# Three heads' values, the chain outputs and the second norm's factors turned by VectorE and by transfers through DRAM

## The chip, the cores and the metric

The kernel runs on one core of one Trainium2 chip. The metric is the device time of one execution in microseconds, the median of several runs. Engines are named as in the profile: PE is TensorE's products, PEld its weight loads, DVE is VectorE, ACT is ScalarE, POOL is GpSimd, SP is SyncE, which issues the DMAs.

## The reference

One layer of a hybrid decoder over a sequence of 1024 tokens of width 1024, all in float32. An RMS norm and one input projection feed two mixers. Mixer A is a gated DeltaNet with four heads of 128; mixer B is an attention with eight heads of 64 over three dilated windows. Their outputs side by side go through one output projection and are added to the input. A second RMS norm follows, a gated MLP of width 2816 with a short causal convolution, and a last RMS norm. Cut to what the change touches:

```python
h = rmsnorm(x, norm1_w)
proj = h @ w_in
qkv_a = silu(causal_dwconv(qkv_a, conv_qkv_w))
qa, ka, va = l2norm(q) * 128 ** -0.5, l2norm(k), v
o_a = gated_delta_rule(qa, ka, va, g, beta)          # chunked, a state of 128 x 128 per head
o_a = rmsnorm(o_a, gdn_norm_w) * silu(z)
x = x + concatenate([o_a, o_b], -1) @ w_out
h = rmsnorm(x, norm2_w)
u = causal_dwconv(h @ w_up, ffn_conv_w)
x = x + (silu(gate) * up) @ w_down
return rmsnorm(x, final_norm_w)
```

## The kernel before

**Layout.** Activations lie transposed: 128 channels on the partitions, 1024 tokens along the free dimension. Products of full precision are made of three products of split operands (`mm3`: high times high, high times low, low times high). `half(h)` is a half of 512 tokens. The mixers' chains need some operands by token instead, so tiles of 128 x 128 are transposed by TensorE against an identity matrix (`tp`), which lands in a PSUM bank, and then copied to SBUF.

**What sets the order.** A planner (`Weave`) runs generators, called streams, each with a level; it keeps its own estimate of time for TensorE (`wv.pe`), for each engine and for each tile's readiness. An `Engine` object wraps an engine with a fixed price and a price per element, and for the queues with a time to land: `sy` is the SP queue at 0.05 us, 0.00142 us an element of a partition's row and 2.2 us to land. `wv.need(tile)` is the time until the planner expects the tile; `yield` with that lets other streams go first. The order of TensorE's instructions is fixed to the order in which the streams issue them. The orders of the other engines and of the queues are made by a scheduler with a simulation of its own, where `uv` and `ua` are VectorE and ScalarE with urgency. Every engine works its queue in order. Tiles of one tag share a ring of slots; `t2` is two deep.

**The stages.** `dense` takes the projection's columns in the order of `DENSE`: keys, attention values, then q and v of each head in turn, the attention's columns, and last the gate columns z. Each column is 48 products. Beside it, at more urgent levels, run `kprep`, `qprep` and `vprep` for each head. When the keys of all heads are done, `forward_sub` solves 32 x 32 triangles on VectorE, and `merges` joins them to 128 x 128 in the visits listed in `VISITS` (steps a, b, c, d for each head, with copies `w1` and `w2` in the ring `t2`); a visit waits for its operands and MSLACK more. `chain(h)` then steps through eight chunks of 128 tokens. The state recurrence makes it a sequence of short products and VectorE operations, and the four heads' chains are interleaved. A chain ends with a multiplication by GpSimd, then comes `finish`. `attention` starts when all four outputs are finished. The gate columns z fill TensorE's time beside the attention. `out_proj`, `mlp_up` (with a Strassen scheme of seven products P1 to P7 for each channel tile) and `mlp_down` follow.

**The three places of the change.**
- `vprep(h, vT)`: `tokens` transposes the eight pieces of a head's values and ScalarE scales each with the key norm on its way from PSUM to `vtok`, the tile that the chain reads, and later overwrites with its output.
- `finish(h, osb)`: eight transposes of the head's output, a copy by ScalarE with the norm weight (`gw2`), a store to `mixer[h]` in DRAM. At column z of the head it is read back into `og` and multiplied by the gate.
- `rms2_power` and `rms2_spread`: the sums of squares by token (a product with ones), GpSimd's power, then eight transposes of a factor column broadcast over 128 columns, and two copies to `rstdB`, which holds the factors on every partition. They are called in `up` for the first channel tile: `rms2_power` between P6 and P7, after the last quarter of P2, and `rms2_spread` after P7.

Of the kernel before, what the change touches and what calls it, by code (L numbers as in the profile page):

```python
# [10 lines left out]
OP = mybir.AluOpType  # L11
# [136 lines left out]
def hybrid_layer(tc, I, out):  # L148
# [6 lines left out]
    ua = Engine(wv, nc.scalar, "scalar", 0.12, 0.00085, first=tc.high_priority)  # L155
    po_ = Engine(wv, nc.gpsimd, "gpsimd", 0.15, 0.0021)
    sy = Engine(wv, nc.sync, "sync", 0.05, 0.00142, 2.2)
    sa = Engine(wv, nc.scalar, "actq", 0.05, 0.00142, 2.2)
    es = ExitStack()
    cp = es.enter_context(tc.tile_pool(name="cp", bufs=1))  # L160
# [6 lines left out]
    def tile_(pool, shape, dt, name, tag, bufs):  # L167
        return wv.slot(pool.tile(list(shape), dt, name=name, tag=tag, bufs=bufs), tag, bufs)
# [3 lines left out]
    def A(name, tag, dt=F32, shape=(P, 1024)):  # L172
        if tag in TURNS:
            i = turns[tag] = turns.get(tag, -1) + 1
            tag = TURNS[tag][i % len(TURNS[tag])]
        return tile_(lp, shape, dt, name, tag, SLOTS[tag])
# [19 lines left out]
    def tp(dst, src, idt=None, us=0.11):  # L196
        tc.stamp_issue_order_token(nc.tensor.transpose(dst, src, ident if idt is None else idt).ins, TOKEN)  # L197
        wv.product(us, dst, src)
# [61 lines left out]
    qpark = dp.tile([H, P, S], F32, name="qpark")  # L260
    atpark = dp.tile([H, P, S], F32, name="atpark")
    ddram = dp.tile([7, 8, P], F32, name="ddram")
    xpark = dp.tile([KT, P, S], F32, name="xpark")
    upark = dp.tile([FT, P, S], F32, name="upark")

# [3 lines left out]
    def next_bank(tag, *tiles, slack=0.0):  # L269

        while max(wv.need(*tiles), wv.slot_free(tag, 2)) + slack > 1e-3:
            yield max(wv.need(*tiles), wv.slot_free(tag, 2)) + slack
        return bank(tag)

    def half(i):
        return slice(i * 512, i * 512 + 512)
# [236 lines left out]
    def silu2(xr, name):  # L513
        y = A(name, "ev")
        ac.activation(y, xr, AF.Tanh, scale=0.5)
        ve.scalar_tensor_tensor(y, y, 1.0, xr, op0=OP.add, op1=OP.mult)
        return y
# [15 lines left out]
    def dense():  # L533

        yield from wv.until("first")
        yield from wv.until("norms")
        wv.add(2, first_keys())

        srcs, tiles = [], 0
        for col in DENSE:  # L540
            if col[0] == "V":
                srcs += [I["wv"][j] for j in range(4)]
            else:
                srcs.append(I["wi"][tiles])
                tiles += 1
        place = [0]
        raw = [raw_weight(srcs[0])]
        nxt = [weight(None, st=raw.pop())]
        raw.append(raw_weight(srcs[1]))

        def take():
            w = nxt.pop()
            i = place[0] = place[0] + 1
            if i < len(srcs):
                nxt.append(weight(None, st=raw.pop(), spare=i >= 17))
            if i + 1 < len(srcs):
                raw.append(raw_weight(srcs[i + 1]))
            return w

        def values_by_token(g):  # L560

            banks = [bank(t) for t in ("asc", "asc", "ch", "ch")]
            for j in range(4):
                w = [t.rearrange("p (k m) -> p k m", k=2) for t in take()]
                for kk in range(2):
                    k = 2 * j + kk
                    for i, pt in enumerate(banks):
                        c = 4 * g + i
                        yield wv.need(pt, *w)
                        mm3(pt, [t[:, c * P:(c + 1) * P] for t in xs[k]], [t[:, kk, :] for t in w], k == 0, k == KT - 1)  # L570
            for i in range(0, 4, 2):
                vx = A("vx", "ev", shape=(P, 2, 512))
                for e in range(2):
                    c = 4 * g + i + e
                    ac.activation(vx[:, e, :], banks[i + e], AF.Copy, scale=rst[:, c:c + 1])
                c = 4 * g + i
                sy.dma_start(vpark[c * P:(c + 2) * P].rearrange("(e p) d -> p e d", e=2), vx)
            wv.done.add(("V", g))

        for i, col in enumerate(DENSE):  # L580
            kind, h = col[:2]
            if kind == "V":
                yield from values_by_token(h)
                continue
            if kind == "z":
                yield from wv.until(("o", h))
            w = [t.rearrange("p (k m) -> p k m", k=KT) for t in take()]
            pair = []
            for hh in range(2):
                pt = bank("hf")  # L590
                yield wv.need(pt, *w)
                for k in range(KT):
                    mm3(pt, [t[:, k, :] for t in w], [t[:, half(hh)] for t in xs[k]], k == 0, k == KT - 1)
                    yield 0.0

                pair.append(pt)
                if hh == 0:
                    xr = A("aqkv" if kind == "a" else "xr", "go" if kind == "k" else "ev")
                scaled(pair, "xr", kind == "a", t=xr, hs=(hh,))
            if kind == "k":  # L600
                T["k", h] = conv_silu(xr, 4 + h, "kT", "kT*")
                wv.add(3, kprep(h))
            elif kind == "q":
                q = conv_silu(xr, h, "qT", "qa")
                wv.add(4, qprep(h, q))
            elif kind == "v":
                v = conv_silu(xr, 8 + h, "vT", "qa")
                wv.add(4, vprep(h, v))
            elif kind == "z":
                og = gated[h] = A("og", "kT*")  # L610
                sy.dma_start(og, mixer[h])
                ve.tensor_tensor(og, og, silu2(xr, "zz"), op=OP.mult)
            else:
                sy.dma_start(apark[h, col[2]], xr)
                wv.done.add(col)
        wv.done.add("dense")
# [83 lines left out]
    def qprep(h, qT):  # L700
# [22 lines left out]
        d.update(rq=rq, gq=gq)  # L723
        wv.done.add(("q", h))

    def vprep(h, vT):
        yield from wv.until(("q", h))
        yield wv.need(vT, slack=SLACK)
        G[h]["vtok"] = yield from tokens(vT, A("vtok", ("dv", "dw")[h % 2]), G[h]["nk"])
        wv.done.add(("v", h))  # L730

    def forward_sub():
# [179 lines left out]
        wv.add(1, finish(h, vtok))  # L912

    def finish(h, osb):
        for hh in range(2):
            pt = yield from next_bank("atr", osb)
            for c in range(4):
                i = 4 * hh + c
                tp(pt[:, c * P:(c + 1) * P], osb[:, i * P:(i + 1) * P])
            ot = tile_(sp, [P, 512], F32, "ot", "t2", 2)  # L920
            ac.activation(ot, pt, AF.Copy, scale=gw2)
            sy.dma_start(mixer[h][:, half(hh)], ot)
        wv.done.add(("o", h))


# [21 lines left out]
    def attention():  # L947
# [56 lines left out]
        def turn(pair):  # L1004
# [26 lines left out]
            if g["n"] < 7 and pair[1]["u"] == 3:  # L1031
                dt = tile_(sp, [P, 32], F32, "dt", "dt", 2)
                ve.transpose(dt, dns[g["n"] % 2])
                to = ddram[g["n"]]
                for b in range(4):
                    sy.dma_start(to[:, 32 * b:32 * b + 32], dt[32 * b:32 * b + 8, :])
                rT = g["rT"] = tile_(sp, [P, 512], F32, "rT", "t2", 2)
                for e, er in enumerate(HALVES):
                    src = to.rearrange("(u e) t -> e u t", e=2)[e]
                    sy.dma_start(rT[er].rearrange("p (u t) -> p u t", u=4),  # L1040
                                 bass.AP(tensor=src.tensor, offset=src.offset, ap=[[0, 64]] + list(src.ap)))

        def spread(pair):
# [216 lines left out]
    def rms2_power():  # L1260
        ps = bank("atr")
        for c in range(NCH):
            mm(ps[:, c:c + 1], rstdB[:, c * P:(c + 1) * P], ones[:, :1], 0.215)
        rs = sp.tile([P, NCH], F32, name="rs")
        uv.tensor_scalar(rs, ps[:, :NCH], 1.0 / 1024, EPS, op0=OP.mult, op1=OP.add)
        rsqrt(rs, rs, NCH)
        return rs

    def rms2_spread(rs):
        for h in range(2):  # L1270
            pb = bank("atr")
            for c in range(4):
                tp(pb[:, c * P:(c + 1) * P], rs[:, 4 * h + c:4 * h + c + 1].to_broadcast([P, P]))
            ve.tensor_copy(rstdB[:, half(h)], pb)

    W = {}
    raws = {}
# [62 lines left out]
    def up(n, before):  # L1340
# [15 lines left out]
        u2 = tile_(wp, [P, 512], F32, "u2", "wlo", 2)  # L1356
        last["u2"] = ac.activation(u2, pa, AF.Copy)
        if before is None:
            yield from up_product(n, "P2", pd, False, ks=(3,))
            rs = rms2_power()  # L1360
        else:
            yield from up_product(n, "P5", pc, True, False)
        yield from up_product(n, "P7", pa, False, False)
        if before is None:
            rms2_spread(rs)
        else:
            pd = yield from next_bank("hf")
            yield from up_product(n, "P2", pd)
# [346 lines left out]
```

## Time and profile before

| | us |
|---|---|
| median of 3 runs (1196.92 to 1198.09) | 1197.95 |
| the profiled execution's own time | 1197.51 |
| its span in the trace | 1195.7 |
| TensorE busy | 1183.8 |
| VectorE busy | 915.7 |
| ScalarE busy | 571.0 |
| GpSimd busy | 82.1 |
| granted TensorE clock, mean | 0.997 |

Busy times are sums over one profiled execution. The span runs from its first to its last instruction; the execution's own time is a little longer. A group's row gives line, engine, operation, written tile and read tiles with their shapes, the count, then busy time in us and mean duration in ns, then the idle time of the engine just before, with what ended it. A row of the timeline gives start, duration, engine, line and instruction. Most rows of VectorE and ScalarE have line 142 or 144, those of the wrapper, and TensorE's 193 (products) and 197 (transposes), so rows are found by tile names.

### The profile page before, as it was taken

The page shows a single profiled execution, that of the slowest core. Times are in us where ns is not written, and L with a number is a line of the kernel's source. Part 1 is how long each engine was busy: PE and PEld are TensorE (multiplying, and loading weights), DVE is VectorE, ACT ScalarE, POOL GpSimd, SP SyncE. Part 2 cuts the span into 40 slices and gives each one's busy share as a digit, 9 for nine tenths or more (in the row PEclk, how much of TensorE's full clock was granted, in tenths as well). Part 3 has the DMA queues.
Part 4 walks back from the last instruction along what each step waited for, and adds up shares of the span by engine and source line. Part 5 has one row for each costly group of instructions (what it writes and reads, how often), then busy time and mean ns, then how long its engine had stood idle before and what let it go on. Part 6 is the DMA issues. An engine that isn't in the chain of part 4 may idle for free.

```text
span 1195.7 us, 18255 instructions
## 1 busy us (share of the span) xinstructions
PE 1183.8 (99%) x7022; PEld 978.6 (82%) x7022; DVE 915.7 (77%) x1457; ACT 571.0 (48%) x1119; POOL 82.1 (7%) x74
## 2 busy tenths in 40 slices
PE   9999999999999999999999999999999999999997
PEld 6888888888777778888888888888888888888886
DVE  7683975665365665777989898989888889999875
ACT  7375345355444533555545444445444453434441
POOL 0212010214211110000000000000000000000000
PEclk9999999999999999999999999999999999999998
DMA  7435234435644214442212313132231398546514
GB/s 238 107 97 150 80 114 126 153 113 183 224 131 126 90 54 132 159 159 106 89 71 88 101 58 106 53 106 75 85 99 60 120 370 284 194 161 224 161 54 141
DMA packets 90055, 156.67 MB, mean 131 GB/s; under 512 B 21840, under 2 KB 40560, under 8 KB 89968
## 3 DMA queue, kind: packets, MB, share of 16 engines
q1 hardware_dynamic: 89104, 154.72, 39.7%
q8 instruction: 55, 0.90, 0.3%
q10 hardware_dynamic: 864, 0.79, 0.2%
q14 instruction: 32, 0.26, 0.1%
HBM read 119.52 MB, written 35.96 MB: 130 GB/s over the span
## 4 chain that ended last, share of the span: by engine, by line
PE 95%; DVE 2%; ACT 2%; issue 1%; DMA 0%; POOLq 0%; POOL 0%; DVEq 0%; SPq 0%; ACTq 0%
PE ps L193 45%; PE pa L193 20%; PE dw L193 17%; PE pc L193 10%; PE ps L197 2%; DVE kT L142 1%; ACT sm L144 1%; ACT whi L142 0%; DMA xt<-in_xT 0%; DVE x1h L142 0%; PE pd L193 0%; DVE zz L142 0%; ACT dec L142 0%; DVE xr L142 0%; DVE sm L144 0%
## 5 line engine op out<-in xcount | busy, mean ns | idle before, releaser
L193 PE MATMUL dw<-pr 128*128 128x512 f32 (+1 forms) x984 | 211.6, 377 | 0.0
L193 PEld LDWEIGHTS dw<-pr 128*128 128x128 f32 x984 | 176.6, 188 | 34.0 <-ACT xu L142 0.5
L193 PE MATMUL ps<-xhi,whi 128*128 128x512 f32 x384 | 157.0, 409 | 0.8 <-ACT xhi L144 0.8
L193 PE MATMUL ps<-xhi,wlo 128*128 128x512 f32 x384 | 150.0, 391 | 0.0
L193 PE MATMUL ps<-xlo,whi 128*128 128x512 f32 x384 | 148.4, 390 | 0.0
L193 PE MATMUL pa<-T,pair 128*128 128x512 f32 x528 | 127.1, 389 | 0.0
L193 PEld LDWEIGHTS pa<-T,pair 128*128 128x128 f32 x528 | 99.0, 188 | 20.6
L193 PEld LDWEIGHTS ps<-xhi,whi 128*128 128x128 f32 x384 | 72.2, 188 | 19.8 <-issue 5.6
L193 PEld LDWEIGHTS ps<-xhi,wlo 128*128 128x128 f32 x384 | 72.1, 188 | 15.5
L193 PEld LDWEIGHTS ps<-xlo,whi 128*128 128x128 f32 x384 | 72.3, 188 | 12.6
L142 ACT ACTIVATE u<-pa 128x512 f32<-128x512 f32 x44 | 26.3, 598 | 107.3 <-PE pa L193 107.3
L142 DVE SCALAR_TENSOR_TENSOR y<-xu,fcw,y 128x1023 f32<-128x1023 f32 (+1 forms) x44 | 56.3, 1280 | 22.1 <-ACT y L142 22.0
L142 ACT ACTIVATE whi<-wst 128x1024 fp32r<-128x1024 f32 x36 | 38.2, 1063 | 65.7 <-PE ps L193 49.0
L193 PE MATMUL pa<-B,A 128*128 128x512 f32 x264 | 63.4, 389 | 0.0
L193 PE MATMUL pc<-T,S 128*128 128x512 f32 x264 | 63.4, 389 | 0.0
L193 PE MATMUL pa<-T,S 128*128 128x512 f32 x264 | 63.4, 389 | 0.0
L193 PE MATMUL pc<-B,pair 128*128 128x512 f32 x264 | 63.4, 389 | 0.0
L142 DVE TENSOR_TENSOR wst<-wst 128x512 f32<-128x512 f32 x88 | 60.4, 686 | 0.9
L193 PE MATMUL ps<-B,pair 128*128 128x512 f32 x252 | 60.5, 389 | 0.0
L142 ACT ACTIVATE pr<-r 128x1024 fp32r<-128x1024 f32 (+1 forms) x44 | 36.2, 838 | 45.7 <-PE dw L193 31.3
L193 PEld LDWEIGHTS pa<-T,S 128*128 128x128 f32 x264 | 49.5, 188 | 10.3
L193 PEld LDWEIGHTS pc<-B,pair 128*128 128x128 f32 x264 | 49.5, 188 | 10.3
(251 smaller groups left out, 2327.3 us busy)
## 6 DMA issues: line engine op xcount, KB each, us to landing
wst<-in_wu SPq DMA_DIRECT2D x44, 512.0 KB, 3.6
wd<-in_wd SPq DMA_DIRECT2D x44, 512.0 KB, 4.3
upark<-y SPq DMA_DIRECT2D x22, 512.0 KB, 4.6
wst<-in_wi SPq DMA_DIRECT2D x21, 512.0 KB, 3.9
r<-upark SPq DMA_DIRECT2D x11, 512.0 KB, 9.2
r<-upark SPq DMA_DIRECT2D x22, 256.0 KB, 5.9
wa<-in_wd SPq DMA_DIRECT2D x22, 256.0 KB, 2.9
wst<-in_wv SPq DMA_DIRECT2D x8, 512.0 KB
```

The lines of the kernel that those rows point to most:

```text
L142: return getattr(eng, op)(*a, **kw)
L144: return getattr(eng, op)(*a, **kw)
L193: tc.stamp_issue_order_token(nc.tensor.matmul(dst, lhs, rhs, start=start, stop=stop, **kw).ins, TOKEN)
L197: tc.stamp_issue_order_token(nc.tensor.transpose(dst, src, ident if idt is None else idt).ins, TOKEN)
```

## The change

Two new helpers turn a 128 x 1024 tile through DRAM. `blocks_out` lets VectorE transpose each 128 x 128 piece in its sixteen blocks of 32 x 32, eight instructions in two halves of 512 columns, each half in a tile of the ring `t2`; eight DMAs store them so that the blocks come to lie at their transposed places in DRAM. `blocks_in` reads the result back in four DMAs. A new `Engine` object `sq` stands for such small DMAs on the same SP queue, with a lower price for the planner (0.05 us, 0.00036 us an element and 0.4 us to land).

- `vprep`: for heads 0, 1 and 2 the values go through `blocks_out` and `blocks_in`, and ScalarE scales `vtok` in place. Head 3 keeps TensorE's transposes.
- `finish`: `blocks_out` of the chain's output to `odram`, for all four heads. At column z `blocks_in` reads it into `og`, and the norm weight's factor is applied in the multiplication with the gate.
- `rms2_power`: the factors are turned by one VectorE transpose of 128 x 32, stored in four small DMAs and broadcast to `rstdB` by one DMA; `rms2_spread` goes. In `up` it comes right after P6, and the last quarter of P2 comes after P7.
- The attention's small stores of denominators and their read-back, on the SP queue as before, go by `sq` too.

```diff
+    sq = Engine(wv, nc.sync, "small", 0.05, 0.00036, 0.4)
...
+    ndram = dp.tile([S], F32, name="ndram")
+    odram = dp.tile([H, 32, 4 * S], F32, name="odram")
+    vdram = dp.tile([3, 32, 4 * S], F32, name="vdram")
...
                 og = gated[h] = A("og", "kT*")
-                sy.dma_start(og, mixer[h])
-                ve.tensor_tensor(og, og, silu2(xr, "zz"), op=OP.mult)
+                blocks_in(og, odram[h])
+                ve.scalar_tensor_tensor(og, og, gw2, silu2(xr, "zz"), op0=OP.mult, op1=OP.mult)
...
+    def blocks_out(src, dst):
+        for hh in range(2):
+            bt = tile_(sp, [P, 512], F32, "bt", "t2", 2)
+            for c in range(4):
+                ve.transpose(bt[:, c * P:c * P + P], src[:, (4 * hh + c) * P:(4 * hh + c + 1) * P])
+            to = dst.rearrange("j (f b i) -> b j f i", f=32, b=4)[:, :, 16 * hh:16 * hh + 16]
+            for b in range(4):
+                sq.dma_start(to[b], bt[32 * b:32 * b + 32].rearrange("p (f i) -> p f i", i=32))
+
+    def blocks_in(dst, src):
+        of = src.rearrange("j (c a t) -> a j c t", c=NCH, a=4)
+        for a in range(4):
+            sq.dma_start(v8(dst)[32 * a:32 * a + 32], of[a])
+
     def vprep(h, vT):
         yield from wv.until(("q", h))
         yield wv.need(vT, slack=SLACK)
-        G[h]["vtok"] = yield from tokens(vT, A("vtok", ("dv", "dw")[h % 2]), G[h]["nk"])
+        vtok = G[h]["vtok"] = A("vtok", ("dv", "dw")[h % 2])
+        if h == 3:
+            yield from tokens(vT, vtok, G[h]["nk"])
+        else:
+            blocks_out(vT, vdram[h])
+            blocks_in(vtok, vdram[h])
+            yield wv.need(vtok, slack=-1.0)
+            for c in range(NCH):
+                cs = slice(c * P, (c + 1) * P)
+                ua.activation(vtok[:, cs], vtok[:, cs], AF.Copy, scale=G[h]["nk"][:, c:c + 1])
         wv.done.add(("v", h))
...
     def finish(h, osb):
-        for hh in range(2):
-            pt = yield from next_bank("atr", osb)
-            for c in range(4):
-                i = 4 * hh + c
-                tp(pt[:, c * P:(c + 1) * P], osb[:, i * P:(i + 1) * P])
-            ot = tile_(sp, [P, 512], F32, "ot", "t2", 2)
-            ac.activation(ot, pt, AF.Copy, scale=gw2)
-            sy.dma_start(mixer[h][:, half(hh)], ot)
+        yield wv.need(osb)
+        blocks_out(osb, odram[h])
         wv.done.add(("o", h))
...
-        rs = sp.tile([P, NCH], F32, name="rs")
-        uv.tensor_scalar(rs, ps[:, :NCH], 1.0 / 1024, EPS, op0=OP.mult, op1=OP.add)
-        rsqrt(rs, rs, NCH)
-        return rs
-
-    def rms2_spread(rs):
-        for h in range(2):
-            pb = bank("atr")
-            for c in range(4):
-                tp(pb[:, c * P:(c + 1) * P], rs[:, 4 * h + c:4 * h + c + 1].to_broadcast([P, P]))
-            ve.tensor_copy(rstdB[:, half(h)], pb)
+        rs = tile_(sp, [P, 32], F32, "rs", "dt", 2)
+        ve.memset(rs, 1.0)
+        uv.tensor_scalar(rs[:, :NCH], ps[:, :NCH], 1.0 / 1024, EPS, op0=OP.mult, op1=OP.add)
+        rsqrt(rs[:, :NCH], rs[:, :NCH], NCH)
+        dt = tile_(sp, [P, 32], F32, "dt", "dt", 2)
+        uv.transpose(dt, rs)
+        to = ndram.rearrange("(c t) -> c t", c=NCH)
+        for b in range(4):
+            sq.dma_start(to[:, 32 * b:32 * b + 32], dt[32 * b:32 * b + NCH, :])
+        sy.dma_start(rstdB, bass.AP(tensor=ndram.tensor, offset=ndram.offset, ap=[[0, P]] + list(ndram.ap)))
...
         if before is None:
-            yield from up_product(n, "P2", pd, False, ks=(3,))
-            rs = rms2_power()
+            rms2_power()
         else:
             yield from up_product(n, "P5", pc, True, False)
         yield from up_product(n, "P7", pa, False, False)
         if before is None:
-            rms2_spread(rs)
+            yield from up_product(n, "P2", pd, False, ks=(3,))
```

More of the change, by code (lines that the diff above doesn't have):

```diff
@@ L1035, in turn @@
                 for b in range(4):
-                    sy.dma_start(to[:, 32 * b:32 * b + 32], dt[32 * b:32 * b + 8, :])
+                    sq.dma_start(to[:, 32 * b:32 * b + 32], dt[32 * b:32 * b + 8, :])
                 rT = g["rT"] = tile_(sp, [P, 512], F32, "rT", "t2", 2)
@@ L1039, in turn @@
                     src = to.rearrange("(u e) t -> e u t", e=2)[e]
-                    sy.dma_start(rT[er].rearrange("p (u t) -> p u t", u=4),
+                    sq.dma_start(rT[er].rearrange("p (u t) -> p u t", u=4),
                                  bass.AP(tensor=src.tensor, offset=src.offset, ap=[[0, 64]] + list(src.ap)))
```

## The prediction

> **What bounds the kernel now.** I read the page's busy shares and its chain first, then busy time by stage, then the groups and single rows of the transposes that go, and last what else stands on VectorE, ScalarE and SP at those places.
>
> ```profile
> span 1195.7 us, 18255 instructions
> PE 1183.8 (99%) x7022; PEld 978.6 (82%) x7022; DVE 915.7 (77%) x1457; ACT 571.0 (48%) x1119; POOL 82.1 (7%) x74
> PE 95%; DVE 2%; ACT 2%; issue 1%; DMA 0%; POOLq 0%; POOL 0%; DVEq 0%; SPq 0%; ACTq 0%
> 20.00:560.00 540.00, 537.90 (x4098) 441.20 (x4097) 349.79 (x766) 268.89 (x726) 75.37 (x53) 1.00 0.42 129
> 560.00:900.00 340.00, 340.00 (x1513) 281.84 (x1512) 299.98 (x343) 163.87 (x216) 2.06 (x1) 1.00 0.25 83
> ```
>
> The two last rows are stages: length, then PE, PEld, DVE, ACT and POOL busy, granted clock, DMA share, GB/s. TensorE is busy 537.9 of 540 us in the stage where nearly all of the change lies, at clock 1.00, and the chain is 95% PE. So an instruction taken from TensorE is worth its issue time there, and every wait that the change puts in TensorE's fixed order costs its full length, because no spare time is left to take it up. VectorE (300 of 340 us in the up-projection) and the DMA queues (share 0.42) are filled less.
>
> **What goes: 64 transposes on TensorE.** 24 of values (three heads by eight), 32 of chain outputs, 8 of the second norm.
>
> ```profile
> 147.74 0.40 PE L193 MATMUL ps<-xhi,wlo 128*128 128x512 f32 x1
> 147.97 1.04 PE L197 MATMUL ps<-ident,vT 128*128 128x128 f32 x8
> 148.76 0.48 PE L193 MATMUL ps<-xhi,whi 128*128 128x512 f32 x1
> 149.08 0.39 PE L193 MATMUL ps<-xlo,whi 128*128 128x512 f32 x1
> 149.31 0.39 PE L193 MATMUL ps<-xhi,wlo 128*128 128x512 f32 x1
> L197 PE MATMUL ps<-ident,vT 128*128 128x128 f32 x32 | 4.2, 274 | 0.0
> L197 PE MATMUL ps<-ident,vtok 128*128 128x128 f32 x32 | 4.5, 273 | 0.1
> L197 PE MATMUL ps<-ident,rs 128*128 128x128 f32 x16 | 2.7, 294 | 1.1 <-POOL rs L142 1.1
> ```
>
> The first five rows are start, duration, instruction. From 147.74 to 149.31, 1.57 us pass; three dense products at their own spacing (149.08 to 149.31, 0.23) would take 0.68, so eight transposes cost 0.89 us. Eight groups of eight: 7.1 us. The busy times of the three groups give another bound: 24 x 4.2/32 + 32 x 4.5/32 + 8 x 2.7/16 = 9.0 us, which counts ends that overlap the neighbours. I take 7.1, worked from starts, and keep 9.0 for the low end.
>
> The second norm gives a little back. Before, its transposes stand between the products P7 and P4 while ScalarE copies P7's bank (`u3`), which P4 then adds to.
>
> ```profile
> 565.64 1.29 PE L193 MATMUL pa<-T,pair 128*128 128x512 f32 x5
> 566.77 1.03 PE L197 MATMUL ps<-ident,rs 128*128 128x128 f32 x8
> 567.68 1.65 PE L193 MATMUL pa<-T,pair 128*128 128x512 f32 x6
> 567.03 0.60 ACT L142 ACTIVATE u<-pa 128x512 f32<-128x512 f32 x1 [1.29 <-PE pa L193]
> ```
>
> P7's last product starts near 566.55 (565.64 plus four spacings), the copy ends at 567.63 and P4 starts at 567.68: 1.13 us. The three products of P2 moved there fill 4 x 0.23 = 0.9, so 0.2 us of waiting remains. Net 7.1 - 0.2 = 6.9.
>
> **What is added to VectorE and ScalarE.** 57 turns: 7 x 8 of 128x128 and one of 128x32.
>
> ```profile
> L142 DVE STREAM_TRANSPOSE dt<-dn 128x32 f32<-128x32 f32 x7 | 1.5, 212 | 0.3
> L144 DVE COPY pt<-ps 128x256 f32<-128x256 f32 x28 | 11.6, 414 | 3.9 <-PE ps L197 3.8
> L144 DVE COPY pb<-ps 128x128 f32<-128x128 f32 x12 | 3.3, 275 | 0.0
> 140.00:172.00 32.00, 32.00 (x167) 27.21 (x166) 29.64 (x65) 12.56 (x39) 4.92 (x3) 1.00 0.34 115
> ```
>
> 128 columns more cost a copy 414 - 275 = 139 ns, so a 128x128 turn is about 212 + 104 = 0.32 us: 2.5 us a head, 17.7 us in all. Only the first head's 2.5 us meet a full VectorE (29.6 of 32 us, the forward substitution among it). That delays the substitution's end, and its results' loads:
>
> ```profile
> L142 SPq DMA_DIRECT2D um<-xtdram x16: 432/449/487, 174.9 to 184.4; - x16
> DMA to landing us min/median/max: 1.8/2.0/2.3
> 185.23 0.69 PE L193 MATMUL ps<-x,um 32*32 32x32 f32 x32
> ```
>
> The first head's four `um` pieces are issued by 176.7 and landed by 178.7; TensorE reads them at 185.23. Six us of cover hide 2.5 us; without it they would be TensorE's loss. ScalarE loses eight copies of 128x512, which costs and gains nothing on the path. The gate's factor moves into an operation that runs anyway.
>
> **What is added on the queue.** A head writes 8 transfers of 512 pieces of 128 B and reads back 4 of 128 KB in pieces of 512 B. The solved triangles go just so in the kernel before: `um` 256 pieces of 128 B, `x` 512.
>
> ```profile
> x<-xdram SPq DMA_DIRECT2D x8, 64.0 KB, 2.6
> vn<-vpark SPq DMA_DIRECT2D x16, 128.0 KB, 2.7
> ```
>
> So after the first four turns (1.3): 8 issues of 0.45 and the landing, 3.6 + 2.6; four reads at the same 0.45, 1.8 + 2.7. Together 12.0 us from the source to the turned tile. The planner that fixes TensorE's order charges it less (`sq`: 0.05 + 512 x 0.00036 = 0.23 an issue and 0.4 to land; 0.42 a read): 0.8 + 1.9 + 0.4 + 1.7 + 0.4 = 5.2. Who reads the tiles decides what the 6.8 us of difference cost:
>
> ```profile
> 194.10 1.06 ACT L142 ACTIVATE vT<-vT 128x1024 f32<-128x1024 f32 x1 [1.29 <-DVE vT L142]
> L193 PEld LDWEIGHTS ps<-vtok,um x8: 187/192/192, 238.3 to 243.4; 128*128 128x128 f32 x8
> L142 DVE TENSOR_TENSOR og<-og,zz x4: 1203/1224/1225, 421.1 to 467.1; 128x1024 f32<-128x1024 f32 x4
> L142 POOL TENSOR_TENSOR vtok<-vtok,ms x4: 1897/1898/1899, 280.7 to 306.4; 128x1024 f32<-128x1024 f32 x4
> 572.14 1.22 DVE L142 TENSOR_TENSOR xu<-xu,rstdB 128x1024 f32<-128x1024 f32 x1
> 573.35 1.23 DVE L142 TENSOR_TENSOR pair<-wst,pair 128x1024 fp32r<-128x1024 f32 x1
> 586.85 1.52 PE L193 MATMUL pa<-T,pair 128*128 128x512 f32 x6
> 564.50 2.06 POOL L142 TENSOR_TENSOR rs<-rs,mhalf 128x8 f32<-128x8 f32 x1 [124.90 <-DVE rs L144]
> dec<-gdram SPq DMA_DIRECT2D x4, 512.0 KB, 6.1
> ```
>
> Values: the third head's are made at 195.2, so turned near 207, and the chains start at 238.3: 30 us of cover. Chain outputs: the last is made at 308.3, so ready near 321, and used from 421.1 on: 100 us of cover. Without the covers each would cost its 12 us. Norm factors: the power starts 0.7 us earlier than at 564.50, since P2's three products now follow; power 2.1, turn 0.2, four issues of 0.45, a landing of 2.0 and the broadcast 6.1 (that of `dec`, the same size and kind): 576.0, 3.9 us behind VectorE's use of them at 572.14. VectorE's next step there, half of the next channel tile's weights (573.35 to 574.58), is first read by the P4 of 586.85, so 12 us cover 3.9; uncovered it is 3.9 of TensorE.
>
> SP's 89 new issues (84 and 5) of 0.45 are some 40 us spread over the span, 5.4 a head; behind them stand the weights, one dense column ahead (48 products of 0.23, 11 us). A read-back also waits 2.6 us on SP for its writes. The lead covers these 8.0 us; without it TensorE would wait them out for weights.
>
> **Where something comes back: the merges.** The third head's turned halves take two slots of the ring `t2`, two deep, in which the merges keep `w1` and `w2`.
>
> ```profile
> L142 ACT ACTIVATE w<-ps x8: 374/486/595, 186.0 to 216.4; 32x256 f32<-32x256 f32 x4, 64x512 f32<-64x512 f32 x4
> ```
>
> Eight copies in 30 us, one every 4, each read by the next visit of TensorE. A half holds its slot for 4 x 0.45 + 2.0 = 3.8 us after its turns, both halves for 5.6; the planner charges 8 x 0.23 + 0.4 = 2.3 and puts the visit 1.5 us (MSLACK) after the copy. One visit comes 5.6 - 2.3 - 1.5 = 1.8 us early, and TensorE waits. Bounds: 0 if the halves fall between two uses, 3.6 if two visits are hit. I take 1.8, since visits are about as dense as the holds are long.
>
> **Sum.** Against the profiled execution, 1197.51 us (span 1195.7 and 1.8 around it): -7.1 + 0.2 + 1.8 = -5.1, 1192.4. The median of the runs, 1197.95, lies 0.44 above it: 1192.9 us.
>
> [...] The rows above give 0.32 us for a 128x128 turn by VectorE and 0.89/8 = 0.11 for one by TensorE: 0.21 more. [...]
>
> **Rivals.**
> 1. All is covered, nothing comes back at the ring: 1197.95 - 6.9 = 1191.1. For it: the 30 and 100 us of cover. Against: merges' copies every 4 us.
> 2. ScalarE is held by the third head's scalings. They are urgent and queued in a fixed order; put where the planner's charge has them, 1 us early, they hold ScalarE 6.8 + 1.0 = 7.8 us for the transfers, and the merges' copies stand behind. Less MSLACK, TensorE waits 6.3: 6.9 - 6.3 gives 1197.4, no difference. If SP comes late to the pieces too, it is slower:
>
> ```profile
> SPq L142 <- DVE wlo L142: 61.1, 16, 15.0
> ```
>
> SP stands 61.1/16 = 3.8 us on average (15.0 at most) for a weight's slot. 7.8 + 3.8 - 1.5 = 10.1 lost, 1201.2. It decides once ScalarE is held over 6.9 + 1.5 = 8.4 us. For it: the planner's charge is under half of the transfers' time. Against: the queues are ordered with a simulation of their own, and TensorE waits for no DMA so far.
> 3. The small pieces clog the queue for the weights.
>
> ```profile
> DMA packets 8589, 1.11 MB, mean 79 GB/s; under 512 B 8574, under 2 KB 8574, under 8 KB 8589
> q1 hardware_dynamic: 8589, 1.11, 48.5%
> ```
>
> In the 14 us from 172, 8589 small packets and some weights took 48.5%: at most 6.8 us, 0.8 ns a packet, 3.2 us for a head's 4096. That leaves a column's lead of 11 us intact; if the pieces took four times that, 13 us, 2 us of each of seven heads would show: 1197.95 - 6.9 + 14 = 1205.1. [...]
>
> **How the numbers follow.** About 0.2% (2.4 us) can be told from no change. Forecast 0.40, rival 1 0.22, rival 2 without difference 0.11, its slower form 0.20, rival 3 with whatever else makes TensorE wait 0.07. Faster 0.62, same 0.11, slower 0.27. The range goes from 1189.0 (the busy-time bound, 1197.95 - 9.0) to 1201.5, just past the price of rival 2's slower form; rival 3 and longer waits stay out. The faster cases' own range is 1189.0 to 1195.
>
> **What would show it.** Right: 64 fewer PE transposes; STREAM_TRANSPOSE 128x128 near 0.32; `vdram` and `odram` landing in 2 to 3 us; TensorE's waits under 3 us beside the merges; `xu` times `rstdB` some 4 us later with no PE wait after. Wrong: ScalarE waiting on DMA for `vtok` over 8 us, or TensorE waiting for weights between 145 and 215, or for a chain step between 280 and 310 where VectorE's turns stand before a chain's operation.

## The result, and the profile after

The changed kernel takes 1212.62 us (median of 5 runs, 1210.38 to 1216.62) where the kernel before takes 1197.95: 1.0123 times as long, 95% interval 1.0111 to 1.0135. It is slower by some 14.7 us. 1192.9 was forecast, with a range to 1201.5.

| us | before | after |
|---|---|---|
| profiled execution, its own time | 1197.51 | 1216.62 |
| span | 1195.7 | 1214.6 |
| TensorE busy | 1183.8 | 1186.9 |
| TensorE not busy (span less busy) | 11.9 | 27.7 |
| mean granted clock | 0.997 | 0.990 |
| first product of the output projection | 463.6 | 479.7 |
| first P4 of the up-projection | 567.7 | 583.1 |

The profiled execution of after is the longest of its five, 4 us over the median, so not all of its losses need be the change's: some 3 us lie at the border between up- and down-projection (980 to 1000), where ScalarE waits 5.6 us for a read of parked data. The rest of the table is what the median has to explain.

The page of after, the lines that were shown of before:

```profile
span 1214.6 us, 18303 instructions
PE 1186.9 (98%) x6958; PEld 978.3 (81%) x6958; DVE 925.5 (76%) x1513; ACT 566.5 (47%) x1111; POOL 82.0 (7%) x74
PE 85%; DVE 5%; ACT 3%; DMA 2%; SPq 2%; issue 2%; POOLq 0%; POOL 0%; DVEq 0%; ACTq 0%
```

TensorE issues 64 products fewer (6958 against 7022), as it should, and is busy 3.1 us *longer*. That points to its clock. Its share of the chain falls from 95 to 85%. By stages, of after (length; PE, PEld, DVE, ACT and POOL busy; granted clock, DMA share, GB/s), and one row of before:

```profile
20.00:560.00 540.00, 523.34 (x3969) 426.87 (x3968) 345.47 (x802) 252.59 (x700) 75.26 (x53) 0.99 0.45 131
190.00:240.00 50.00, 40.70 (x548) 33.33 (x547) 21.50 (x45) 20.26 (x57) 8.69 (x4) 0.86 0.46 126
200.00:205.00 5.00, 1.31 (x76) 1.06 (x76) 1.79 (x6) 3.84 (x12) 0.00 (x0) 0.85 0.47 154
205.00:210.00 5.00, 4.67 (x23) 4.00 (x24) 1.03 (x3) 1.44 (x4) 0.00 (x0) 0.50 0.28 107
220.00:225.00 5.00, 1.19 (x50) 0.90 (x50) 1.73 (x3) 1.77 (x3) 0.00 (x0) 0.89 0.77 202
225.00:230.00 5.00, 4.70 (x37) 3.90 (x38) 1.10 (x2) 1.98 (x6) 0.00 (x0) 0.50 0.39 105
284.00:320.00 36.00, 32.01 (x191) 27.52 (x192) 21.57 (x72) 14.27 (x56) 15.97 (x10) 1.00 0.80 197
560.00:900.00 340.00, 339.93 (x1508) 281.33 (x1507) 299.32 (x348) 166.88 (x223) 2.06 (x1) 1.00 0.27 87
```

```profile
190.00:240.00 50.00, 50.00 (x613) 42.08 (x596) 29.34 (x49) 22.87 (x68) 10.41 (x5) 1.00 0.41 137
284.00:320.00 36.00, 35.88 (x203) 30.40 (x202) 11.18 (x31) 14.72 (x36) 14.99 (x10) 1.00 0.70 225
```

The 50 us of the merges hold most of the loss: 9.3 us without work, and two stretches in which the clock is 0.50. The first comes right behind the idle of 200 to 205, the second behind that of 220 to 225. The account is best made at the output projection, where all the columns of the input projection are done, in whatever order. It starts 16.1 us late although seven groups of transposes (7 x 0.89 = 6.2 us) have gone before it: 22.3 us lost. From 20 to 560 TensorE is without work for 16.7 us, before for 2.1: 14.6 more, 9.3 of it beside the merges and 3.9 between 284 and 320, where the turns of the chain outputs stand. The two stretches at half clock last 6.8 us each (203.46 to 210.29 and 223.94 to 230.77), with TensorE busy for 6.0 and 5.5 of them; by estimate they lose half of that, 5.8 together, since TensorE's dense products start 0.43 us apart there (207.79 to 209.93) and 0.23 at full clock (210.56 to 211.95). 14.6 and 5.8 make 20.4; 1.9 I can't place. The change of the norm then gains 0.7 (16.1 to 15.4).

### The profile page after: what moved, and what is told of

The parts are those of the page before. It is cut to its first block, busy times and chain, and to the rows that moved or that the text cites. A ratio compares the mean times of both kernels' runs of the same rounds, so it can differ in the third digit from the quotient of the medians.

```text
span 1214.6 us, 18303 instructions
## 1 busy us (share of the span) xinstructions
PE 1186.9 (98%) x6958; PEld 978.3 (81%) x6958; DVE 925.5 (76%) x1513; ACT 566.5 (47%) x1111; POOL 82.0 (7%) x74
## 4 chain that ended last, share of the span: by engine, by line
PE 85%; DVE 5%; ACT 3%; DMA 2%; SPq 2%; issue 2%; POOLq 0%; POOL 0%; DVEq 0%; ACTq 0%
PE ps L194 38%; PE pa L194 19%; PE dw L194 17%; PE pc L194 10%; SPq L142 2%; PE ps L198 2%; DMA r<-upark 1%; ACT sm L144 1%; DVE kT L142 1%; ACT whi L142 1%; DVE vT L142 1%; DVE bt L142 1%; DMA vtok<-vdram 1%; DMA vdram<-bt 1%; ACT vtok L144 0%
## 5 line engine op out<-in xcount | busy, mean ns | idle before, releaser
L194 PEld LDWEIGHTS ps<-xhi,wlo 128*128 128x128 f32 x384 | 72.7, 189 | 15.8
L194 PEld LDWEIGHTS pc<-T,S 128*128 128x128 f32 x264 | 49.6, 188 | 10.3
```

The source lines that it names most:

```text
L194: tc.stamp_issue_order_token(nc.tensor.matmul(dst, lhs, rhs, start=start, stop=stop, **kw).ins, TOKEN)
```

## Where the time goes in the changed kernel

**The merges.** The waits of after from 140 to 240 (us in total, times, longest), then single rows of its timeline:

```profile
ACT vtok L144 <- DMA vtok<-vdram: 15.7, 3, 7.0
ACT w L142 <- DMA vdram<-bt: 9.2, 2, 6.3
PE ps L194 <- ACT w L142: 8.2, 3, 3.6
200.27 2.44 ACT L144 ACTIVATE vtok<-vtok,nk 128x128 f32<-128x128 f32 x8 [6.82 <-DMA vtok<-vdram]
202.74 0.37 ACT L142 ACTIVATE w<-ps 32x256 f32<-32x256 f32 x1
203.17 0.24 PE L194 MATMUL ps<-um,w 32*32 32x32 f32 x2 [3.57 <-ACT w L142]
220.28 0.37 ACT L142 ACTIVATE w<-ps 32x256 f32<-32x256 f32 x1 [6.32 <-DMA vdram<-bt]
224.66 0.59 ACT L142 ACTIVATE w<-ps 64x512 f32<-64x512 f32 x1 [2.90 <-DMA vdram<-bt]
225.30 0.36 PE L194 MATMUL ps<-um,w 64*64 64x64 f32 x1 [3.18 <-ACT w L142]
```

Two different things hold ScalarE there, and both end in the same wait of TensorE, for the merges' copy `w`.

At 193.5 ScalarE reaches the *second* head's scalings and stands 6.82 us for the read-back; the scalings take 2.44; the copy behind them comes at 202.74, and TensorE, idle since 199.6, goes on. Why the read-back is late shows on SP (start, duration, count):

```profile
180.42 2.04 SPq L142 DMA_DIRECT2D x<-xdram  x4
182.50 5.45 SPq L142 DMA_DIRECT2D um<-xtdram  x8
188.06 2.51 SPq L142 DMA_DIRECT2D x<-xdram  x4
190.62 4.64 SPq L142 DMA_DIRECT2D um<-xtdram  x8
195.30 2.50 SPq L142 DMA_DIRECT2D vtok<-vdram  x4
```

The head's last stores were issued by 179.8. Its read-back is issued from 195.3 on, behind 24 loads of solved triangles that fill SP for 15 us.

At 214 it is the *third* head: its turns are to take both slots of the ring `t2`, and the copies `w` that come after them in the ring wait 6.32 and 2.90 us for the stores to land. ScalarE reaches the first of them at 213.96, when VectorE has not even begun the turns (215.26, behind a convolution of `qT`). A 1.91 us wait for that head's own read-back follows.

**The chain outputs.** Four rows of the timeline:

```profile
301.02 0.89 DVE L142 STREAM_TRANSPOSE bt<-vtok 128x128 f32<-128x128 f32 x4 [1.78 <-DMA odram<-bt]
303.06 0.49 PE L194 MATMUL ps<-ct,kT 128*128 128x128 f32 x2 [2.20 <-DVE ct L144]
311.67 1.62 DVE L142 STREAM_TRANSPOSE bt<-vtok 128x128 f32<-128x128 f32 x8
313.94 0.49 PE L194 MATMUL ps<-wke,ktok 128*128 128x128 f32 x2 [0.97 <-ACT w L144]
```

VectorE waits 1.78 us for a slot with a turn at the head of its queue; the chain's own step `ct` stands behind that, and TensorE waits 2.20 for it. At 311.67 eight turns stand in front of the chain's `wke` (313.21), for which ScalarE's `w` and then TensorE wait: 0.97 more.

**The norm.** The factors arrive late and nobody but VectorE notices:

```profile
584.50 0.34 SPq L142 DMA_DIRECT2D rstdB<-ndram  x1
588.42 1.22 DVE L142 TENSOR_TENSOR xu<-xu,rstdB 128x1024 f32<-128x1024 f32 x1 [1.39 <-DMA rstdB<-ndram]
```

## The experiments

Two theories of the loss. **A**: ScalarE is held beside the merges, by the scalings that wait for a read-back and by the ring `t2`; each stop is made dearer by the clock behind it. **B**: every head that goes through DRAM costs something by itself on SP and the queue. A third, **C**: the first head's turns delay the forward substitution and with it the triangles' loads.

**One place at a time.** The other two places as before, and the attention's small transfers by `sy` as before in all three; so the lower price that `sq` gives these was not run alone.

> Only the three heads' values are turned by VectorE and transfers; chain outputs, the second norm and the attention's small stores are as before. Theory A (the loss sits where values are turned beside the merges: ScalarE is held at the scalings by the read-back, the merges' copies wait for the ring t2, TensorE idles 3.7 us twice and its granted clock is halved for some 5 us after each): 1198 + 11.7 = 1209 to 1211, chains' first product near 250, two stretches at clock 0.50 between 200 and 235. Theory B (the loss is the small transfers' load on the one queue, alike for each of the seven heads, 21.6 / 7 = 3.1 us a head): 1198 + 3 x 3.1 - 2.7 = 1204 to 1205.

> Only the four chain outputs are turned by VectorE and transfers; the rest is as before. Theory A: the transposes saved (3.6 us) are outweighed by VectorE's turns that stand in front of the other heads' chain steps, one of them waiting for a slot of t2: 1198 + 2 to 5, 1200 to 1203, with TensorE's waits of 2 us and less on VectorE or ScalarE between the chains' start and end, and no drop of the clock. Theory B: 1198 + 4 x 3.1 - 3.6 = 1206 to 1207.

> Only the second norm's factors are turned by VectorE and transfers, with P2's last quarter after P7; the rest is as before. Both theories: TensorE's eight transposes go and 0.2 us of waiting stays, 1197.3, which 5 rounds can hardly tell from 1198; xu times rstdB is some 4 us later and TensorE doesn't wait for it. If it is slower by over 1 us, both are incomplete.

| only | us | ratio to before (1197.64) |
|---|---|---|
| values, three heads | 1210.99 | 1.0114 [1.0100, 1.0127] |
| chain outputs, four heads | 1199.84 | 1.0015 [1.0004, 1.0025] |
| norm | 1197.86 | 1.0002 [0.9993, 1.0011] |

+13.4, +2.2 and +0.2 make 15.8 against 14.7 measured. Three heads of values cost six times what four heads of outputs cost: theory B does not hold. The norm's 0.7 us of TensorE don't show in its median.

**A deeper ring.** If the ring is the hold, a third slot should end it. (`ba`, `zt` and `az` share slots to make room.)

```diff
-            bt = tile_(sp, [P, 512], F32, "bt", "t2", 2)
+            bt = tile_(sp, [P, 512], F32, "bt", "t2", 3)
...
-    ba = sp.tile([P, NCH, 8], F32, name="ba")
+    ba = tile_(sp, [P, NCH, 8], F32, "ba", "w2", 1)
```

> The whole change, with the ring t2 three deep instead of two (three small tiles of the gates share slots of other tags to make room). Theory A: the merges' copies no longer wait for the turned halves' stores (6.3 and 2.9 us of ScalarE in the changed kernel), so the second idle stretch near 220 and its slow clock go, some 6 us, and the wait of 2.2 us near 302 too: 1204 to 1207. The first stretch near 200, where ScalarE waits 6.8 us at the second head's scalings, stays. Theory B: as the changed kernel, 1211 to 1214.

1217.56, 1.0159 [1.0145, 1.0173]: a miss, slower than the change itself. Its waits from 140 to 250, and a row of its timeline:

```profile
ACT vtok L144 <- DMA vtok<-vdram: 17.2, 3, 7.3
PE ps L194 <- ACT w L142: 8.0, 2, 5.0
226.16 2.44 ACT L144 ACTIVATE vtok<-vtok,nk 128x128 f32<-128x128 f32 x8 [3.73 <-DMA vtok<-vdram]
```

The wait of `w` for `vdram<-bt` is gone, so the ring's part of A was seen rightly. But now the third head's scalings are reached 3.73 us before their data, in front of the last merges' copies, and TensorE's longest wait grows from 3.6 to 5.0. Taking one hold away moved the stop to the next in line: from 190 to 240 TensorE is without work for 9.1 us, against 9.3. That the run is slower than the change itself comes from the attention: from 320 to 460 TensorE is without work for 4.3 us, against 1.3, and the granted clock has a mean of 0.98 there, against 1.00. What stops it there I did not follow.

**The first head alone.** Its turns are the ones that delay the substitution; it comes before the merges.

```diff
-        if h == 3:
+        if h:
             yield from tokens(vT, vtok, G[h]["nk"])
```

> As the kernel with only the values changed, but only the first head goes by transfers; heads 1 to 3 keep TensorE's transposes. Theory A (what costs is ScalarE's order beside the merges, which the second and third head meet and the first doesn't): 1197.6 - 0.9 = 1196.7, between 1196 and 1198.5. Theory B (each head by transfers costs alike, 13.4 / 3 us): 1202. Theory C (the turns and stores delay the triangles and their loads, and with them the merges; the first head's 1.7 us of turns in the middle of the substitution do that too): 1199 to 1202.

1199.91, 1.0014 [1.0006, 1.0023]. So the 13.4 us are not the first head's; theory C is out as the main cause. But the run should have gained 0.9 and lost 2.3: it lies outside theory A's range and inside theory C's, so this head has a price of some 3 us that A does not cover. ScalarE is held here too, 7.61 us for the read-back at 161.1; TensorE's visible waits from 140 to 190 add to 0.9, and the clock stays at 1.00. The other part of the 3 us is not explained.

**The scalings behind the merges.** The values alone; a head's scalings wait for the last merges' copy, so ScalarE can't reach them early.

```diff
             yield wv.need(vtok, slack=-1.0)
+            yield from wv.until(("m", H - 1))
             for c in range(NCH):
                 cs = slice(c * P, (c + 1) * P)
-                ua.activation(vtok[:, cs], vtok[:, cs], AF.Copy, scale=G[h]["nk"][:, c:c + 1])
+                after(ua.activation(vtok[:, cs], vtok[:, cs], AF.Copy, scale=G[h]["nk"][:, c:c + 1]), last["w2"], ...)
```

> As the kernel with only the values changed, but the scalings of the three heads' values by ScalarE are ordered behind the last of the merges' copies w2, so that no copy can stand behind them. Theory A: the stretch in which ScalarE waits 6.7 us for the second head's read-back goes, with its idle time and slow clock (5.2 us idle and 2.5 to 3.5 of clock); the stretch in which copies wait for the ring t2 (6.0 and 1.2 us on ScalarE) stays: 1211.0 - 8 = 1203, between 1201 and 1205. Theory C: TensorE waits just as long for the merges' operands, 1209 to 1212.

1202.61, 1.0040 [1.0027, 1.0053]: 8.4 us come back, as theory A has it. One stop is left, that of the ring (its timeline, and its stage of the merges):

```profile
211.84 0.38 ACT L142 ACTIVATE w<-ps 32x256 f32<-32x256 f32 x1 [5.43 <-DMA vdram<-bt]
190.00:240.00 50.00, 46.85 (x586) 38.53 (x585) 26.88 (x51) 22.83 (x62) 9.04 (x4) 0.93 0.58 163
```

**And no ring.** The same, with VectorE turning the value tile in place, so that no slot of `t2` is taken:

```diff
-            bt = tile_(sp, [P, 512], F32, "bt", "t2", 2)
+            bt = src[:, half(hh)]
             for c in range(4):
-                ve.transpose(bt[:, c * P:c * P + P], src[:, (4 * hh + c) * P:(4 * hh + c + 1) * P])
+                ve.transpose(bt[:, c * P:c * P + P], bt[:, c * P:c * P + P])
```

> As the kernel with only the values changed, scalings behind the merges' copies, and VectorE turns the pieces in place instead of into the ring t2, so that no copy waits for a store either. Theory A: both stretches go and the transposes saved show: 1197.6 - 2.7 = 1194.9, between 1194 and 1197.5. Theory C: the delays of the triangles' loads behind the stores on SP remain, 1200 or more.

1196.09, 0.9990 [0.9982, 0.9999]: another 6.5 us, and now 1.5 under the kernel before. The same turns, the same transfers, the same 24 triangle loads in front of the second head's read-back (178.3 to 193.0); only what stands behind the wait on ScalarE and the ring has changed. So the delays that theory C names cost at most some 1.2 us here, since 1194.9 was expected. Its row of the merges' stretch:

```profile
190.00:240.00 50.00, 49.31 (x615) 40.99 (x615) 27.86 (x51) 24.17 (x65) 11.38 (x5) 1.00 0.61 177
```

The clock is 1.00 again. Of the 14.9 us between the values alone and this kernel, 8.4 went with the scalings' place and 6.5 with the ring, removed in this order; the other way round, in the whole change with the deeper ring, the ring alone gave nothing.

**The planner's price.** The prediction named as a reason for its rival that the planner charges a small transfer less than half of its time.

```diff
-    sq = Engine(wv, nc.sync, "small", 0.05, 0.00036, 0.4)
+    sq = Engine(wv, nc.sync, "small", 0.45, 0.0, 2.2)
```

> The whole change with one number altered: the planner charges a small transfer what the trace shows, 0.45 us an issue whatever its pieces and 2.2 us to land (before 0.05 + 0.00036 a piece, and 0.4). Rival P (the low charge alone is why ScalarE is held: the orders come from a simulation that believes it): the holds go and the time falls to 1196 to 1200. Theory A (the read-back is late because it stands behind 24 loads of triangles on SP, and the scalings are put by their urgency, which the charge changes little): the holds shorten, but one of the two idle stretches remains: 1203 to 1210.

1211.26, 1.0115 [1.0101, 1.0129]. No gain beyond 1.4 us; the price alone is not the cause, and even theory A's 1203 to 1210 was too hopeful. ScalarE's waits of this run:

```profile
ACT vtok L144 <- DMA vtok<-vdram: 19.9, 3, 7.6
ACT w L142 <- DMA vdram<-bt: 1.1, 1, 1.1
201.76 2.45 ACT L144 ACTIVATE vtok<-vtok,nk 128x128 f32<-128x128 f32 x8 [7.46 <-DMA vtok<-vdram]
217.36 2.44 ACT L144 ACTIVATE vtok<-vtok,nk 128x128 f32<-128x128 f32 x8 [4.90 <-DMA vtok<-vdram]
```

With the price nearer the trace the ring's hold nearly goes, but the scalings keep their place in ScalarE's queue and wait longer than ever. So the price did not put them there; the urgency set in the code (`slack=-1.0`, `ua`) is left as the likely reason, which no run changed by itself.

**The chain outputs.** Outputs alone lose 2.2 where 3.6 (four groups of 0.9) should have been gained. Turning in place was tried here first:

> As the kernel with only the chain outputs changed, but VectorE turns the pieces in place instead of into the ring t2. Theory A: no turn waits for a slot in front of a chain's step or of the attention's operations: 1199.8 - 2 to 3 = 1197 to 1198; the turns of 1.7 us themselves still stand in front of chain steps, so the full 3.6 us saved don't show. If the waits for slots cost nothing, it stays at 1199.8.

1202.07, 1.0038 [1.0023, 1.0053]: a miss. The output lies in the rings `dv` and `dw`, which the attention's `sm` takes over; in place it is held until the stores have landed (the trace is of an execution of 1199.70; ten executions ran from 1199.36 to 1207.89, and what makes the longer ones is not seen in it):

```profile
329.08 0.46 DVE L144 CUSTOM_DVE_ANT_0 sm<-ps,mk 128x288 f32<-128x288 f32 x1 [5.14 <-DMA odram<-vtok]
```

In the run with outputs alone another wait is the longest (its timeline; SP, VectorE, TensorE, then two stages):

```profile
331.98 1.37 SPq L142 DMA_DIRECT2D ddram<-dt  x4
338.19 1.29 SPq L142 DMA_DIRECT2D rT<-ddram  x2
342.37 1.06 DVE L142 TENSOR_TENSOR oT<-ps,rT 128x512 f32<-128x512 f32 x1 [6.43 <-issue]
344.75 0.46 PE L198 MATMUL ps<-ident,sm 64*128 64x64 f32 x8 [2.56 <-ACT sm L144]
340.00:345.00 5.00, 2.44 (x18) 1.75 (x16) 2.63 (x8) 1.04 (x3) 0.00 (x0) 1.00 0.27 93
345.00:350.00 5.00, 4.45 (x54) 3.60 (x52) 3.39 (x13) 3.73 (x13) 2.29 (x1) 0.69 0.30 112
```

The attention's denominators make a small trip through DRAM themselves (`ddram`, then `rT`). Here 4.8 us lie between the last store and the read; before it was 1.4, and the last head's pieces and its read-back had just been put on the same queue. For VectorE's 6.43 us the profile names no releaser; `oT` reads `rT`, whose read-back was issued up to 339.5. ScalarE's `sm`, for which TensorE waits, needs a maximum that VectorE takes behind `oT`. Theory **D**: that is the price of the last head, not of all four. So only the first three go through DRAM, the last is transposed by TensorE:

```diff
     def finish(h, osb):
-        yield wv.need(osb)
-        blocks_out(osb, odram[h])
+        if h == H - 1:
+            ...   # TensorE's transposes, a copy without gw2, a store to mixer[h]
+        else:
+            yield wv.need(osb)
+            blocks_out(osb, odram[h])
```

> Chain outputs alone, and of these only the first three heads through DRAM; the last head's is turned by TensorE as in the kernel before. Theory D (the last head's 4096 pieces and its read-back stand on the queue in front of the attention's first small round trip, ddram to rT; VectorE's oT waited 6.4 us for it at 342 and TensorE stood 2.6 us, then ran at a lower clock): without it three heads save 3 x 0.9 = 2.7 and lose the 1.0 us at 285 to 290: 1197.6 - 2.7 + 1.0 = 1195.9 (1195.2 to 1197.0). Rival (every head costs alike, 5.8 us over four heads): 1197.6 - 2.7 + 4.3 = 1199.2.

1196.21, 0.9986 [0.9977, 0.9995], near the 1195.9 of theory D: 3.6 us better than four heads, with one group of transposes more. But a second thing differs between the two runs: this one was built from the whole change, so the attention's small transfers go by `sq`, where with outputs alone they go by `sy`. How much of the 3.6 us is the last head's, and how much the planner's other price for just that trip, is not separated.

**The whole change, with the values mended.** All three places, the values as in the two edits above (the outputs keep the ring).

> The whole change (values, chain outputs, norm), with two edits to the values alone: a head's scalings stand behind the last merges' copies on ScalarE, and VectorE turns the value tile in place, so no half takes a slot of ring t2. Theory A (ScalarE held by the read-backs and by the ring beside the merges, then the halved clock, is what the whole change lost): the values part was 1196.1 so, the chain outputs add 2.2 and the norm 0.2 by their own runs: 1198.5 (1197.3 to 1200.0). Rival (the pieces of values, outputs and norm load one queue together, so the parts cost more in company): 1203 or more.

> The values with the same two edits, and the second norm's turn; chain outputs by TensorE as in the kernel before. Theory A: 1196.1 + 0.2 = 1196.3 (1195.3 to 1197.3), under the kernel before. Rival (the late scalings only won by the luck of one order): 1198 or more.

The whole: 1194.14, 0.9974 [0.9965, 0.9982], faster than both kernels and the best that was run. Without the outputs: 1196.56, 0.9990 [0.9981, 0.9999], as expected. The whole was expected at 1198.5, from 1197.3 to 1200.0, and came out under that. The two runs differ by the outputs alone, which gain 2.4 us here where they lost 2.2 by themselves. In this kernel the attention's read-back is nearly as late (stores to 332.2, read at 336.32; without the outputs 1.0 us lies between them), yet VectorE waits 2.64 us for it, not 6.43, and TensorE from 320 to 350 for nothing. The outputs' own price at the chains stays, 36.00 us with 34.08 busy from 284 to 320. So four heads on the queue make the read-back late, as theory D has it, but that it must cost time does not follow: it is a matter of what TensorE has beside it. Whether the mended values or the price `sq` made the order that covers it here is not shown.

## Why the prediction was wrong

- **The bound.** Right: TensorE has no spare time, every wait costs its full length. Two of them cost more, by the clock behind them (0.50 for 6.8 us each), for which the sum had no term.
- **What goes.** 64 products went. Where nothing else is hurt the gain arrives: the mended whole has TensorE busy 1177.9 us against 1183.8, and is 3.6 faster in the medians.
- **The turns on VectorE.** Mis-sized, too high: 0.32 us each was worked out, eight take 1.66 us, 0.21 each:

```profile
145.68 1.66 DVE L142 STREAM_TRANSPOSE bt<-vT 128x128 f32<-128x128 f32 x8
```

- **VectorE's load** was not the price: in the mended whole the same 57 turns stand on VectorE (busy 925.4 us, before 915.7), and it is faster than the kernel before.
- **The path of a head.** 12.0 us from the source to the turned tile. The first head's is 13.4 (145.68 to 159.07). For the second it was far too low, since the path was added up as though SP were free. The prediction counted what SP's new issues delay, and not what the new issues themselves stand behind, though it quoted 16 of those loads.
- **Where something comes back: the merges.** This is the step that failed. It charged 1.8 us, with bounds of 0 and 3.6, for one hold, the ring by the third head. The runs show two: the ring, 6.5 us, and the scalings of a head behind its read-back, 8.4 us, both with the clock's share in them, in place of the 1.8. The ring was the right mechanism with the wrong size. A half's hold was nearly right: reckoned 3.8 us after its turns, measured 4.1 (turned by 216.14, the copy free at 220.28). But the copy's wait was counted from the turns, and ScalarE stood there 2.2 us before they were done.
- **Rival 2** had the other half: ScalarE held by scalings, 7.8 us, or 11.6 with SP late, decided by the third head. It was the second head (6.82 us of wait and 2.44 of scalings), and it came beside the ring, not in its stead. Its highest price, 10.1 us of loss, had no term for the clock. It was given a chance of 0.31, of which 0.20 for the slower form; and the reason named for it, the planner's charge, was not the cause.
- **The values' cover of 30 us** was true of the chains, and beside the point: the first to wait was not the tile's reader but whatever stood behind its wait on ScalarE.
- **The chain outputs.** The cover of 100 us held, `og` was in place long before its use. What was written as a sign of being wrong, turns before a chain's operation, is what happened: 2.20 and 0.97 us.
- **The norm.** Right in kind: the factors late, covered, no wait of TensorE. The lateness was mis-sized: 3.9 us were reckoned, VectorE waits 1.39, since the broadcast took 3.9 us (584.50 to 588.4) and not the 6.1 of `dec`. Too small to be measured by itself.
- **Rival 3** did not come in the form of weights that are late. A queue did delay another transfer, the attention's trip, in the run with outputs alone. There eight issues of a head's pieces took 7.4 and 9.2 us on SP, where 0.45 each was counted.

## What to carry to other kernels

Where an engine takes its work in a fixed order, as ScalarE did here with 6.82 us of wait in front of a copy, the cover of a late tile is not the time until its reader needs it, but the time until the *next instruction on that engine* is needed: give a wait for a transfer a place behind the work that others depend on, or an engine that nobody waits for. When a chain of transfers is added up, look at what already stands on the issuing queue at that moment, row by row. And a stop of a full TensorE can cost nearly twice its length (here 3.57 us and, by estimate, 3.0 at half clock behind it), so a change worth a few microseconds of it can't afford one.

## What was not expected of the hardware

**The clock after a stop.** In stages of 1 us around the first stop of after:

```profile
199.00:200.00 1.00, 0.60 (x6) 0.14 (x4) 0.00 (x0) 0.00 (x0) 0.00 (x0) 1.00 1.08 381
202.00:203.00 1.00, 0.00 (x0) 0.00 (x0) 0.00 (x0) 0.98 (x4) 0.00 (x0) 1.00 0.49 201
203.00:204.00 1.00, 0.61 (x36) 0.50 (x38) 0.82 (x3) 0.86 (x3) 0.00 (x0) 0.73 0.00 0
209.00:210.00 1.00, 1.00 (x4) 0.73 (x3) 0.00 (x0) 0.00 (x0) 0.00 (x0) 0.50 0.00 0
210.00:211.00 1.00, 1.00 (x5) 0.82 (x4) 0.01 (x1) 0.24 (x1) 0.00 (x0) 0.85 0.00 0
```

TensorE stands from 199.6 to 203.2; the granted clock falls to 0.50 at 203.46 and is back at full at 210.29, 6.8 us later. TensorE is busy for 6.0 of these and so loses, by estimate, 3.0, nearly as much as by the stop of 3.57 us itself; such losses are what made its busy time grow. The stop of 2.20 us at 303 changed nothing (the stage of 284 to 320 is at 1.00); one of 2.56 us in the run with outputs alone, with more gaps after it, gave a mean of 0.69 over the next 5 us. And in the run with late scalings the clock fell with no single wait of TensorE over 1.6 us. Before it fell, just behind 214, TensorE was busy for 1.19 of 2 us, in part with small products of the merges:

```profile
212.00:214.00 2.00, 1.19 (x50) 0.90 (x50) 1.20 (x3) 1.27 (x2) 0.00 (x0) 1.00 0.99 175
214.00:216.00 2.00, 0.76 (x14) 0.76 (x16) 0.00 (x0) 1.34 (x3) 0.00 (x0) 0.53 0.65 258
216.00:218.00 2.00, 2.00 (x24) 1.79 (x21) 1.10 (x2) 0.59 (x1) 0.00 (x0) 0.50 0.58 161
```

So it is not the longest wait alone that decides. In the trace of after, between 20 and 1180 us, three stretches are at 0.50: 6.83 us from 203.46, 6.83 from 223.94 and 3.41 from 991.94. The 3.41 us just before each of these, and two other stretches as long, at 217.12 and 299.04, behind which the clock stayed at 1.00 for the next 3.41 us:

```profile
200.05:203.46 3.41, 0.24 (x2) 0.13 (x2) 0.31 (x1) 3.14 (x10) 0.00 (x0) 1.00 0.65 215
220.53:223.94 3.41, 1.19 (x50) 0.90 (x50) 1.20 (x3) 1.18 (x2) 0.00 (x0) 1.00 0.94 244
988.53:991.94 3.41, 1.61 (x8) 1.02 (x7) 0.71 (x1) 2.29 (x3) 0.00 (x0) 1.00 1.05 396
217.12:220.53 3.41, 2.11 (x10) 1.41 (x8) 3.38 (x7) 0.25 (x1) 0.00 (x0) 1.00 0.99 223
299.04:302.45 3.41, 1.82 (x13) 1.47 (x11) 1.63 (x6) 0.94 (x4) 0.00 (x0) 1.00 0.75 127
```

TensorE was busy for 0.24 to 1.61 us in front of the three falls, for 1.82 and 2.11 where none followed. What decides between these the runs don't tell.

**A turn by VectorE** of 128 x 128 takes 0.21 us in a row of eight (the 1.66 us at 145.68), near twice what TensorE's own takes (0.89/8 = 0.11). In the run with outputs turned in place it wrote over its source, eight in 1.63 us:

```profile
314.32 1.63 DVE L142 STREAM_TRANSPOSE vtok<-vtok 128x128 f32<-128x128 f32 x8
```
